# A Winograd up projection whose weight sums are formed by accumulating DMAs instead of VectorE

## The chip, the core and the metric

The kernel runs on one core of a Trainium2 chip. The metric is the device time of one execution in microseconds (us). An execution is profiled on the same core; all times of single instructions below come from that profiled execution and count from the first instruction of its span.

## The reference, cut to what matters

One decoder layer on 512 tokens of width 1024 in float32: two kinds of attention, cross attention to 256 memory tokens, then the MLP, which is all that the change touches:

```
a = square(relu(rms_norm(h, g_mlp) @ w_up))     # w_up:   1024 x 4096
h = h + a @ w_down                              # w_down: 4096 x 1024
return rms_norm(h, g_final)
```

## The kernel before, in words

**Products.** A float32 operand is kept as the sum of two float32r parts, hi and lo, and every matrix product is three matmuls (`mm3`, lines 102 to 104): hi times hi, hi times lo, lo times hi. Weights come in pieces of 128 x 1024 elements (512 KB). A piece is loaded by a DMA of SyncE's queue (`load`, line 122), split by `parts` into hi (a copy on ScalarE, line 109) and lo (a subtraction on VectorE, line 113), and then used by TensorE. The tiles hi and lo have three buffers each, shared by all pieces in the order of their use. So the split of a piece can begin when TensorE has done the piece three places ahead of it, and TensorE has two pieces to work on meanwhile.

**The up projection** is done in eight groups, numbered 0 to 7 here. A group is one 2 x 2 block problem (two blocks of 256 features, two of 512 inputs, two of 256 tokens) done with Winograd's seven products in place of eight. With A11 to A22 the four weight blocks of 512 KB (feature block, input block), the weight operands of the seven products are, in their order

```
p1: A11   p5: S1 = A21 + A22   p2: A12   p6: S2 = S1 - A11   p3: S4 = A12 - S2   p4: A22   p7: S3 = A11 - A21
```

`up_items` (line 967) makes them: each block is loaded once, and the four sums S1, S2, S4 and S3 are `tensor_tensor` instructions of VectorE (lines 983, 991, 995, 1002). S2 takes the place of S1 in the tile `s`. The tiles `blk` and `s` share seven buffers (`BLK`), of which a group takes five. The activation operands (sums of token blocks) are made once, ahead of group 0. `product` (line 1079) is 24 matmuls of 128 x 256; `up_group` adds the products up on VectorE, and `put` squares and splits the result.

**The order.** Groups 0 and 1 run one after the other; groups 2, 4 and 6 are woven with the down projection of an earlier quarter (a product, a piece of `w_down`, a product, and so on; a down piece is 24 matmuls of 128 x 512 in the tiles `mm` and `sc`); groups 3, 5 and 7 stand alone again, each behind a woven one. Products rotate over four PSUM banks named `tr` and `av`. The order on ScalarE, VectorE and GpSimd is set by the framework's scheduler; each engine and each DMA queue then runs its instructions strictly in that order. GpSimd has next to nothing to do in the MLP: the few small instructions of `up_norm` in group 0.

Of the kernel before, what the change touches and what calls it, by code (L numbers as in the profile page):

```python
# [10 lines left out]
F32 = mybir.dt.float32  # L11
# [4 lines left out]
ALU = mybir.AluOpType  # L16
AX = mybir.AxisListType

P = 128
# [4 lines left out]
# pairs of feature tiles of a quarter in the order in which the up projection makes them  # L24
DOWN = (0, 2, 1, 3)
EPS = 1e-6
# PE microseconds of filler work after each half of a step, per unit
# [12 lines left out]
# ROPE_THETA ** (-arange(0, 16, 2) / 16) in float32  # L40
# [5 lines left out]
def two_pi_parts(bits, n):  # L46
    """2 pi as a sum of n floats of the given number of bits each."""
    from decimal import Decimal, getcontext

    getcontext().prec = 60  # L50
    rest = Decimal("6.28318530717958647692528676655900576839433879875021164194988918")
    parts = []
    for _ in range(n):
        e = math.frexp(float(rest))[1]
        unit = Decimal(2) ** (e - bits)
        q = (rest / unit).to_integral_value(rounding="ROUND_DOWN") * unit
        parts.append(float(q))
        rest -= q
    return parts
# [3 lines left out]
def tile_decoder_layer(  # L63
# [24 lines left out]
    nc = tc.nc  # L88
# [10 lines left out]
    # Every matrix product is the sum of three products of parts: a float32 is the  # L99
    # exact sum of two float32r, a = hi + lo, and lo * lo lies below float32's last place.  # L100
# [5 lines left out]
    def split(hi, lo, src, scale=1.0, eng=None):  # L106
        """hi + lo = src * scale; scale is a number or a column of one per partition."""
        if isinstance(scale, float):
            nc.scalar.activation(hi, src, AF.Copy, bias=0.0, scale=scale)  # L109
        else:  # L110
            nc.scalar.activation(hi, src, AF.Identity, bias=0.0, scale=scale)
        if isinstance(scale, float) and scale == 1.0:
            (eng or nc.vector).tensor_tensor(lo, src, hi.bitcast(F32), ALU.subtract)  # L113
        else:
            nc.vector.scalar_tensor_tensor(lo, src, scale, hi.bitcast(F32), ALU.mult, ALU.subtract)

    # Pieces of weights in the order of their use; each is loaded and split some pieces ahead.
# [25 lines left out]
    def proj_n(act, o, n, last=8, ahead=2):  # L143
        """o = (act @ w)^T for the next 128 columns of weights and an activation with features
        first; what the steps cost on TensorE."""
        whi, wlo = take(ahead)
        for c in range(8):
            if c == last:
                yield None
            mm3(o, (whi[:, c, :], wlo[:, c, :]), (act[0][:, c, :n], act[1][:, c, :n]), c == 0, c == 7)  # L150
            yield 1.3e-3 * n
# [5 lines left out]
    def rsqrt(pool, v, n, name, eng=None):  # L157
        """v ** -0.5 for a few columns: a guess from the exponent and three Newton steps."""
        y = pool.tile([P, n], F32, tag=name, name=name)
        t = pool.tile([P, n], F32, tag=name + "_t", name=name + "_t")  # L160
        eng = eng or nc.vector
        eng.tensor_scalar(y.bitcast(I32), v.bitcast(I32), -0.5, float(0x5F3759DF), ALU.mult, ALU.add)
        for _ in range(3):
            eng.tensor_tensor(t, y, y, ALU.mult)
            if eng is nc.vector:
                eng.scalar_tensor_tensor(t, t, -0.5, v, ALU.mult, ALU.mult)
                eng.scalar_tensor_tensor(y, t, 1.5, y, ALU.add, ALU.mult)
            else:
                eng.tensor_tensor(t, t, v, ALU.mult)
                eng.tensor_scalar(t, t, -0.5, 1.5, ALU.mult, ALU.add)  # L170
                eng.tensor_tensor(y, t, y, ALU.mult)
        return y
# [72 lines left out]
    for i in range(2):  # L245
        m = cp.tile([P, P], BF16, name=f"mask{i}")
        nc.gpsimd.memset(m, 0.0)
        # kept where q - k - i >= 0
        nc.gpsimd.affine_select(m, m, pattern=[[-1, P]], compare_op=ALU.is_ge, fill=NEG,
                                base=-i, channel_multiplier=1)  # L250
        masks.append(m)
# [16 lines left out]
    # A query tile holds two heads of 64 features: q[h] has the two parts of head h below each other,  # L268
    # hi in its own rows; k[h] has hi of head h in both halves, k[2] lo of both heads in their rows.
# [72 lines left out]
    # Work that fills TensorE between the steps of the mixers, in its order.  # L342
# [21 lines left out]
    class Mixer:  # L364
        """One step of a mixer: a head of differential attention, or a pair of stick-breaking heads."""
# [5 lines left out]
        def scores(self, i):  # L371
            """Scores of query block i against the keys up to its end, for both halves of the rows."""
# [38 lines left out]
        def transpose(self, i):  # L411
            """Weights of query block i into blocks i, i + 3, ... (one for each key block)."""
# [67 lines left out]
    def by_key(w, j):  # L480
        """Weights of key block j, and the columns of query tokens they go to."""
        b0 = 11 if j == 3 else 4 * j
        n = 2 if j == 3 else 4 - j
        return w[:, b0:b0 + n, :].rearrange("p b q -> p (b q)"), slice(S - n * P, S)
# [60 lines left out]
    # x with features first waits in DRAM for the residual  # L545
# [27 lines left out]
    # TensorE runs at its full clock only after some microseconds of work  # L573
# [43 lines left out]
    # angles, and their remainders by 2 pi in three steps, each exact  # L617
# [17 lines left out]
    # cos(a) = sin(pi / 2 - |a|)  # L635
# [9 lines left out]
    # the queries and keys of the first mixer are an eighth; put_k makes the keys whole again  # L645
# [28 lines left out]
    # lambda  # L674
# [152 lines left out]
    kx = [xp.tile([P, 8, M], F32R, name=f"kx{i}") for i in range(2)]  # L827
    vx = [xp.tile([P, 2, D], F32R, name=f"vx{i}") for i in range(2)]
    for n in range(8):
# [3 lines left out]
        if n == 1:  # L833
            # scale of the queries, folded into the softmax
# [112 lines left out]
    # The up projection is done in 2 x 2 blocks (of features, of inputs, of tokens) with Winograd's seven  # L947
    # products for eight: for W = A11 .. A22 (feature block, input block) and activations B11 .. B22
    # (input block, token block)
    #   S1 = A21 + A22, S2 = S1 - A11, S3 = A11 - A21, S4 = A12 - S2  # L950
    #   T1 = B12 - B11, T2 = B22 - T1, T3 = B22 - B12, T4 = T2 - B21
    #   U2 = A11 B11 + S2 T2, U3 = U2 + S3 T3
    #   C11 = A11 B11 + A12 B21, C12 = U2 + S1 T1 + S4 B22, C21 = U3 - A22 T4, C22 = U3 + S1 T1
# [13 lines left out]
    def up_items(q, g):  # L967
        blk = {}
        c0 = q * 1024 + g * 256

        def block(i, j):
            c = c0 + 512 * i
            return load(w_up[:, 4 * j:4 * j + 4, c:c + 256], ml, "blk", bufs=BLK)

        def p1():
            blk[11] = block(0, 0)
            return parts(blk[11])

        def p5():
            blk[21] = block(1, 0)  # L980
            blk[22] = block(1, 1)
            blk["s"] = ml.tile([P, 4, 256], F32, tag="blk", bufs=BLK, name="s")
            nc.vector.tensor_tensor(blk["s"], blk[21], blk[22], ALU.add)
            return parts(blk["s"])

        def p2():
            blk[12] = block(0, 1)
            return parts(blk[12])

        def p6():  # L990
            nc.vector.tensor_tensor(blk["s"], blk["s"], blk[11], ALU.subtract)
            return parts(blk["s"])

        def p3():
            nc.vector.tensor_tensor(blk[12], blk[12], blk["s"], ALU.subtract)
            return parts(blk[12])

        def p4():
            return parts(blk[22])

        def p7():
            nc.vector.tensor_tensor(blk[11], blk[11], blk[21], ALU.subtract)
            return parts(blk[11])
# [3 lines left out]
    def weave(a, b):  # L1007
        """Steps of two lists in turn."""
        return [x for pair in itertools.zip_longest(a, b) for x in pair if x is not None]

    # the steps of the MLP: products of the up projection beside pieces of the down projection
# [83 lines left out]
    def up_group(u):  # L1095
# [17 lines left out]
        add(u2, product(t2), p1, ALU.add)  # L1113
        add(u4, u2, p5, ALU.add)
        yield
        add(c12, product(b22), u4, ALU.add)
# [4 lines left out]
        add(u2, product(t3), u2, ALU.add)  # L1121
# [32 lines left out]
    def up_norm():  # L1154
# [3 lines left out]
        # relu(r u)^2 = r^2 relu(u)^2 for r > 0: the square of the scale goes onto the down products  # L1158
# [25 lines left out]
    # the sum of squares of a token and acc * g_final over the columns done  # L1184
# [17 lines left out]
    # h = -0.5 (mean + eps), the part of it that is done  # L1202
# [18 lines left out]
    def root(h):  # L1221
        # (-2 h) ** -0.5: a guess from the exponent and three Newton steps
# [9 lines left out]
    def finish(t, cols, r):  # L1232
        """cols: the columns that are still to be multiplied by g_final."""
# [55 lines left out]
```

## Time and profile before

| | |
|---|---|
| three runs | 797.5, 799.82, 801.35 us; median 799.82 us |
| the profiled execution | span 795.6 us from first to last instruction |
| TensorE busy (matmuls) | 769.2 us, 97% of the span |
| VectorE, ScalarE, GpSimd busy | 553.1, 423.9, 104.7 us |
| mean granted TensorE clock | 0.986 of full speed |
| moved by DMAs | 77.98 MB, of it 73.03 MB read from HBM |
| chain that ended last | TensorE 84%, VectorE 9%, ScalarE 3%, DMA 1% |

The profile gives no other time for the profiled execution than its span; the median of the runs is 4.2 us longer, which is taken as what lies around the span. Matmuls overlap in the pipeline, so the duration of a single one (0.28 us for 128 x 256) is longer than the distance to the next (0.12 us): the pace is read from the starts.

### The profile page before, as it was taken

The page shows a single profiled execution, that of the slowest core. Times are in us where ns is not written, and L with a number is a line of the kernel's source. Part 1 is how long each engine was busy: PE and PEld are TensorE (multiplying, and loading weights), DVE is VectorE, ACT ScalarE, POOL GpSimd, SP SyncE. Part 2 cuts the span into 40 slices and gives each one's busy share as a digit, 9 for nine tenths or more (in the row PEclk, how much of TensorE's full clock was granted, in tenths as well). Part 3 has the DMA queues.
Part 4 walks back from the last instruction along what each step waited for, and adds up shares of the span by engine and source line. Part 5 has one row for each costly group of instructions (what it writes and reads, how often), then busy time and mean ns, then how long its engine had stood idle before and what let it go on. Part 6 is the DMA issues. An engine that isn't in the chain of part 4 may idle for free.

```text
span 795.6 us, 11669 instructions
## 1 busy us (share of the span) xinstructions
PE 769.2 (97%) x4552; PEld 668.1 (84%) x4552; DVE 553.1 (70%) x829; ACT 423.9 (53%) x723; POOL 104.7 (13%) x200
## 2 busy tenths in 40 slices
PE   7997999999979999999999999999999999999996
PEld 6886788877867899888888899888988899889885
DVE  3889877689896874445746989556865486647745
ACT  5646655777756554254535788333543454345622
POOL 7166443420050011000000030000000000000000
PEclk9998999999989999999999999999999999999998
DMA  9522111211113446224361044332334233230402
GB/s 267 164 81 79 54 54 54 75 35 56 50 53 118 148 130 188 82 77 133 102 191 53 27 162 131 106 107 79 114 99 127 86 92 121 80 105 1 133 1 106
DMA packets 83977, 77.98 MB, mean 98 GB/s; under 512 B 2545, under 2 KB 70290, under 8 KB 83922
## 3 DMA queue, kind: packets, MB, share of 16 engines
q1 hardware_dynamic: 83120, 76.16, 30.8%
q0 software_dynamic: 160, 0.13, 0.4%
q8 instruction: 36, 0.59, 0.3%
q10 hardware_dynamic: 642, 0.93, 0.3%
q14 instruction: 19, 0.16, 0.1%
HBM read 73.03 MB, written 4.19 MB: 97 GB/s over the span
## 4 chain that ended last, share of the span: by engine, by line
PE 84%; DVE 9%; ACT 3%; DMA 1%; issue 1%; POOL 0%; SPq 0%; DVEq 0%; ACTq 0%
PE mm L102 14%; PE mm L103 13%; PE mm L104 13%; PE av L102 5%; PE av L103 5%; PE av L104 5%; PE sc L102 4%; PE sc L103 4%; PE sc L104 4%; PE tr L102 4%; PE tr L104 4%; PE tr L103 4%; PE tr L422 1%; DMA raw<-in_w_in_dram 1%; PE av L451 1%
## 5 line engine op out<-in xcount | busy, mean ns | idle before, releaser
L109 ACT ACTIVATE hi<-raw 128x1024 fp32r<-128x1024 f32 x92 | 97.3, 1057 | 77.7 <-PE tr L103 15.2
L113 DVE TENSOR_TENSOR lo<-raw,hi 128x1024 fp32r<-128x1024 f32 x80 | 99.6, 1245 | 44.7 <-ACT hi L109 43.4
L109 ACT ACTIVATE hi<-blk 128x1024 fp32r<-128x1024 f32 x40 | 42.4, 1061 | 70.1 <-PE sc L104 48.3
L102 PE MATMUL mm<-a,hi 128*128 128x512 f32 x160 | 66.6, 416 | 0.2
L113 DVE TENSOR_TENSOR lo<-blk,hi 128x1024 fp32r<-128x1024 f32 x40 | 48.7, 1221 | 25.9 <-ACT hi L109 25.9
L103 PE MATMUL mm<-a,hi 128*128 128x512 f32 x160 | 63.3, 395 | 0.0
L104 PE MATMUL mm<-a,lo 128*128 128x512 f32 x160 | 63.2, 395 | 0.0
L102 PE MATMUL mm<-b,hi 128*128 128x512 f32 x128 | 50.2, 393 | 0.0
L104 PE MATMUL mm<-b,lo 128*128 128x512 f32 x128 | 50.0, 390 | 0.0
L103 PE MATMUL mm<-b,hi 128*128 128x512 f32 x128 | 49.8, 389 | 0.0
L102 PE MATMUL av<-a,hi 128*128 128x256 f32 (+1 forms) x144 | 42.7, 296 | 0.0
L103 PE MATMUL av<-a,hi 128*128 128x256 f32 (+1 forms) x144 | 42.7, 296 | 0.0
L104 PE MATMUL av<-a,lo 128*128 128x256 f32 (+1 forms) x144 | 42.6, 296 | 0.0
L102 PEld LDWEIGHTS mm<-a,hi 128*128 128x128 f32 x160 | 30.1, 188 | 8.7 <-issue 1.6
L102 PE MATMUL tr<-a,hi 128*128 128x256 f32 x128 | 36.2, 283 | 0.0
L104 PE MATMUL tr<-a,lo 128*128 128x256 f32 x128 | 36.2, 283 | 0.0
L103 PE MATMUL tr<-a,hi 128*128 128x256 f32 x128 | 36.2, 283 | 0.0
L104 PEld LDWEIGHTS mm<-a,lo 128*128 128x128 f32 x160 | 30.1, 188 | 6.9
L103 PEld LDWEIGHTS mm<-a,hi 128*128 128x128 f32 x160 | 30.2, 189 | 5.9 <-POOL a L726 0.2
L102 PE MATMUL mm<-hi,a 128*128 128x256 f32 x112 | 34.4, 307 | 0.0
L103 PE MATMUL mm<-lo,a 128*128 128x256 f32 x112 | 32.6, 291 | 0.0
L104 PE MATMUL mm<-hi,a 128*128 128x256 f32 x112 | 32.5, 291 | 0.0
(388 smaller groups left out, 2346.5 us busy)
## 6 DMA issues: line engine op xcount, KB each, us to landing
blk<-in_w_up_dram SPq DMA_DIRECT2D x32, 512.0 KB, 3.7
raw<-in_w_down_dram SPq DMA_DIRECT2D x32, 512.0 KB, 3.3
raw<-in_w_in_dram SPq DMA_DIRECT2D x24, 512.0 KB, 3.8
raw<-in_w_xkv_dram SPq DMA_DIRECT2D x16, 512.0 KB, 3.9
raw<-in_w_out_dram SPq DMA_DIRECT2D x8, 512.0 KB, 4.0
raw<-in_w_xq_dram SPq DMA_DIRECT2D x8, 512.0 KB, 4.0
raw<-in_w_xo_dram SPq DMA_DIRECT2D x8, 512.0 KB, 4.1
x<-in_x_dram SPq DMA_DIRECT2D x4, 512.0 KB, 8.4
```

The source lines that it names most:

```text
L102: nc.tensor.matmul(o, l[0], r[0], start=first, stop=False)
L103: nc.tensor.matmul(o, l[0], r[1], start=False, stop=False)
L104: nc.tensor.matmul(o, l[1], r[0], start=False, stop=last)
L109: nc.scalar.activation(hi, src, AF.Copy, bias=0.0, scale=scale)
L113: (eng or nc.vector).tensor_tensor(lo, src, hi.bitcast(F32), ALU.subtract)
L422: nc.tensor.transpose(tr[:, j, :], self.es[i][:, h, j * P:(j + 1) * P], ident)
L451: nc.tensor.matmul(o[:, cols], vj, w, start=(j == 0 and part == 0), stop=(j == 3 and part == 1))
```

## The change

The four sums leave VectorE. A block is loaded into a tile by SyncE's queue as before, and a second DMA, issued on GpSimd's queue with `accum_op=ALU.add`, adds another block from DRAM onto it. Since only additions are used, the signs of the first feature block are turned: S2, S4 and S3 become S1 + A11, A12 + (S1 + A11) and A11 + A21, and three instructions of `up_group` subtract where they added. S1, S2 and S4 now follow each other in one tile, `blk["s"]`; A22 and A11 are loaded a second time. Comments were also removed.

```diff
-        def block(i, j):
+        def at(i, j):
             c = c0 + 512 * i
-            return load(w_up[:, 4 * j:4 * j + 4, c:c + 256], ml, "blk", bufs=BLK)
+            return w_up[:, 4 * j:4 * j + 4, c:c + 256]
+
+        def block(i, j):
+            return load(at(i, j), ml, "blk", bufs=BLK)
+
+        def add(raw, i, j):
+            nc.gpsimd.dma_start(raw, at(i, j), accum_op=ALU.add)
+            return raw

         def p1():
-            blk[11] = block(0, 0)
-            return parts(blk[11])
+            return parts(block(0, 0))

         def p5():
-            blk[21] = block(1, 0)
-            blk[22] = block(1, 1)
-            blk["s"] = ml.tile([P, 4, 256], F32, tag="blk", bufs=BLK, name="s")
-            nc.vector.tensor_tensor(blk["s"], blk[21], blk[22], ALU.add)
+            blk["s"] = add(block(1, 0), 1, 1)
             return parts(blk["s"])

         def p2():
-            blk[12] = block(0, 1)
-            return parts(blk[12])
+            return parts(block(0, 1))

         def p6():
-            nc.vector.tensor_tensor(blk["s"], blk["s"], blk[11], ALU.subtract)
-            return parts(blk["s"])
+            return parts(add(blk["s"], 0, 0))

         def p3():
-            nc.vector.tensor_tensor(blk[12], blk[12], blk["s"], ALU.subtract)
-            return parts(blk[12])
+            return parts(add(blk["s"], 0, 1))

         def p4():
-            return parts(blk[22])
+            return parts(block(1, 1))

         def p7():
-            nc.vector.tensor_tensor(blk[11], blk[11], blk[21], ALU.subtract)
-            return parts(blk[11])
+            return parts(add(block(0, 0), 1, 0))
...
-        add(u2, product(t2), p1, ALU.add)
+        add(u2, product(t2), p1, ALU.subtract)
...
-        add(c12, product(b22), u4, ALU.add)
+        add(c12, product(b22), u4, ALU.subtract)
...
-        add(u2, product(t3), u2, ALU.add)
+        add(u2, u2, product(t3), ALU.subtract)
```

How the instructions stand on VectorE around p6 and p3 of group 1. Before, `s_4678` is the tile of S1 and S2 of this group, `blk_4744` that of A12 and S4, `lo_4777` and `lo_4807` are the lo parts of p6 and p3:

```order
L991 TENSOR_TENSOR s_4678<-s_4678,blk_4644 128x1024
L1121 TENSOR_TENSOR resid_93<-av_4457,resid_93 128x512
L113 TENSOR_TENSOR lo_4747<-blk_4744,hi_4746 128x1024
L1002 TENSOR_TENSOR blk_4644<-blk_4644,blk_4674 128x1024
L1122 TENSOR_TENSOR resid_93<-resid_93,tr_4456 128x512
L1123 TENSOR_TENSOR resid_93<-resid_93 128x512
L995 TENSOR_TENSOR blk_4744<-blk_4744,s_4678 128x1024
L113 TENSOR_TENSOR lo_4777<-s_4678,hi_4776 128x1024
```

and in the changed kernel, where `blk_4675` is the one tile of S1, S2 and S4, and `lo_4775` and `lo_4805` are the lo parts of p6 and p3:

```order
L113 TENSOR_TENSOR lo_4745<-blk_4742,hi_4744 128x1024
L1123 TENSOR_TENSOR resid_93<-resid_93,tr_4453 128x512
L1124 TENSOR_TENSOR resid_93<-resid_93 128x512
L113 TENSOR_TENSOR lo_4775<-blk_4675,hi_4774 128x1024
L113 TENSOR_TENSOR b1_2770<-resid_93,b0_2769 128x2x256 x2
L1111 TENSOR_TENSOR resid_93<-tr_4453,resid_93 128x512
L1114 TENSOR_TENSOR resid_93<-av_4454,resid_93 128x512
L1115 TENSOR_TENSOR resid_93<-resid_93 128x512
L113 TENSOR_TENSOR lo_4805<-blk_4675,hi_4804 128x1024
L113 TENSOR_TENSOR lo_4840<-blk_4837,hi_4839 128x1024
```

The sums are gone, and p6 and p3 are split from the same tile, so that the DMA that makes S4 must wait until `lo_4775` has read S2.

GpSimd's queue in the MLP held only `up_norm` before (from line 1159 on; the two rows ahead belong to the cross attention):

```order
L841 TENSOR_SCALAR rx_2771<-rsh_3168 128x4
L842 TENSOR_SCALAR nrx_2772<-rsh_3168 128x4
L1159 TENSOR_SCALAR ssh_4096<-ssh_4096 128x4
L162 TENSOR_SCALAR rsm2_4728<-ssh_4096 128x4
L164 TENSOR_TENSOR rsm2_t_4729<-rsm2_4728 128x4
```

and now, from the end of `up_norm` on, holds the additions. `blk_4675` is the sum tile of group 1, `blk_4976` of group 2, `blk_5431` of group 3, `blk_5700` of group 4; `blk_5299` and `blk_5593` are S3 of groups 2 and 3:

```order
L1162 TENSOR_TENSOR r2_4095<-rsm2_4726 128x4
L981 DMA blk_4675<-in_w_up_dram 128x4x256
L981 DMA blk_4976<-in_w_up_dram 128x4x256
L981 DMA blk_4675<-in_w_up_dram 128x4x256
L981 DMA blk_5299<-in_w_up_dram 128x4x256
L981 DMA blk_5431<-in_w_up_dram 128x4x256
L981 DMA blk_4976<-in_w_up_dram 128x4x256 x2
L981 DMA blk_5593<-in_w_up_dram 128x4x256
L981 DMA blk_5700<-in_w_up_dram 128x4x256
L981 DMA blk_5431<-in_w_up_dram 128x4x256 x2
```

The first sum of the next group (S1 of group 2, of group 4) now stands directly ahead of S4 of group 1 and of S2 of group 3 in the same queue.

## Rows read from the trace of the kernel before

**Rows 1.** The page: its span, and busy time, share and instructions by engine.

```profile
span 795.6 us, 11669 instructions
...
PE 769.2 (97%) x4552; PEld 668.1 (84%) x4552; DVE 553.1 (70%) x829; ACT 423.9 (53%) x723; POOL 104.7 (13%) x200
```

**Rows 2.** Table by stage: stretch, length, busy per engine (count), clock, DMA share, GB/s.

```profile
500.00:520.00 20.00, 20.00 (x123) 17.96 (x122) 10.27 (x11) 8.06 (x10) 0.00 (x0) 1.00 0.28 93
...
640.00:660.00 20.00, 20.00 (x170) 20.00 (x170) 16.46 (x19) 11.91 (x16) 0.00 (x0) 1.00 0.37 106
```

**Rows 3.** TensorE's waits over the span: us in total, times, longest.

```profile
PE av L451 <- DVE wt L113: 5.2, 1, 5.2
PE sc L378 <- DVE rt L296: 4.5, 1, 4.5
```

**Rows 4.** Groups by line, VectorE: busy and mean; idle before, by releaser.

```profile
L983 DVE TENSOR_TENSOR s<-blk 128x1024 f32<-128x1024 f32 x8 | 9.8, 1224 | 4.6 <-DMA blk<-in_w_up_dram 3.9 <-DVE lo L113 0.4
```

**Rows 5.** VectorE in order of time: start, us, instruction [idle before].

```profile
444.86 1.23 DVE L113 TENSOR_TENSOR lo<-s,hi 128x1024 fp32r<-128x1024 f32 x1 [0.17 <-ACT hi L109]
...
470.15 1.23 DVE L113 TENSOR_TENSOR lo<-s,hi 128x1024 fp32r<-128x1024 f32 x1 [0.24 <-ACT hi L109]
...
551.28 1.22 DVE L113 TENSOR_TENSOR lo<-s,hi 128x1024 fp32r<-128x1024 f32 x1 [1.00 <-ACT hi L109]
...
562.41 1.22 DVE L113 TENSOR_TENSOR lo<-blk,hi 128x1024 fp32r<-128x1024 f32 x1 [0.20 <-ACT hi L109]
...
593.52 1.23 DVE L113 TENSOR_TENSOR lo<-s,hi 128x1024 fp32r<-128x1024 f32 x1 [4.47 <-ACT hi L109]
```

**Rows 6.** ScalarE in order of time, at the same places.

```profile
453.08 1.06 ACT L109 ACTIVATE hi<-s 128x1024 fp32r<-128x1024 f32 x1 [0.27 <-PE tr L103]
...
474.74 1.06 ACT L109 ACTIVATE hi<-s 128x1024 fp32r<-128x1024 f32 x1 [1.78 <-PE av L103]
...
558.38 1.06 ACT L109 ACTIVATE hi<-s 128x1024 fp32r<-128x1024 f32 x1 [1.69 <-PE tr L103]
...
561.31 1.06 ACT L109 ACTIVATE hi<-blk 128x1024 fp32r<-128x1024 f32 x1 [1.39 <-PE av L103]
...
600.72 1.06 ACT L109 ACTIVATE hi<-blk 128x1024 fp32r<-128x1024 f32 x1 [2.13 <-PE sc L104]
```

**Rows 7.** TensorE: the first matmul of p3 in groups 0, 1 and 3.

```profile
463.31 0.28 PE L102 MATMUL tr<-a,hi 128*128 128x256 f32 x1
...
483.17 0.28 PE L102 MATMUL av<-a,hi 128*128 128x256 f32 x1
...
566.89 0.28 PE L102 MATMUL tr<-a,hi 128*128 128x256 f32 x1
```

**Rows 8.** The page: DMA queues (packets, MB, share); issues (KB, us to landing).

```profile
q1 hardware_dynamic: 83120, 76.16, 30.8%
q0 software_dynamic: 160, 0.13, 0.4%
...
blk<-in_w_up_dram SPq DMA_DIRECT2D x32, 512.0 KB, 3.7
...
lv<-in_lambda_q_dram POOLq DMA_DIRECT2D x2, 32.0 KB, 7.5
```

**Rows 9.** GpSimd in order of time, near the start.

```profile
2.14 0.99 POOL L526 DMA_DIRECT2D pos_i<-in_positions_dram  x1
```

**Rows 10.** Table by stage, behind TensorE's two long waits.

```profile
63.80:68.90 5.10, 5.09 (x23) 4.57 (x24) 4.86 (x7) 3.52 (x8) 3.97 (x3) 0.50 0.00 0
68.90:72.00 3.10, 3.10 (x22) 2.84 (x21) 2.99 (x6) 2.21 (x7) 2.70 (x3) 0.76 0.02 5
...
232.70:236.20 3.50, 3.41 (x11) 3.12 (x12) 3.50 (x7) 0.58 (x1) 0.41 (x2) 0.50 0.00 0
236.20:239.00 2.80, 2.80 (x20) 2.61 (x18) 1.61 (x4) 1.45 (x3) 0.41 (x2) 0.74 0.00 0
```

More of the change, by code (lines that the diff above doesn't have):

```diff
@@ L969, in up_items @@
         c0 = q * 1024 + g * 256
+        def at(i, j):
+            c = c0 + 512 * i
+            return w_up[:, 4 * j:4 * j + 4, c:c + 256]
         def block(i, j):
-            c = c0 + 512 * i
-            return load(w_up[:, 4 * j:4 * j + 4, c:c + 256], ml, "blk", bufs=BLK)
+            return load(at(i, j), ml, "blk", bufs=BLK)
+        def add(raw, i, j):
+            nc.gpsimd.dma_start(raw, at(i, j), accum_op=ALU.add)
+            return raw
         def p1():
-            blk[11] = block(0, 0)
-            return parts(blk[11])
+            return parts(block(0, 0))
         def p5():
-            blk[21] = block(1, 0)
-            blk[22] = block(1, 1)
-            blk["s"] = ml.tile([P, 4, 256], F32, tag="blk", bufs=BLK, name="s")
-            nc.vector.tensor_tensor(blk["s"], blk[21], blk[22], ALU.add)
+            blk["s"] = add(block(1, 0), 1, 1)
             return parts(blk["s"])
         def p2():
-            blk[12] = block(0, 1)
-            return parts(blk[12])
+            return parts(block(0, 1))
         def p6():
-            nc.vector.tensor_tensor(blk["s"], blk["s"], blk[11], ALU.subtract)
-            return parts(blk["s"])
+            return parts(add(blk["s"], 0, 0))
         def p3():
-            nc.vector.tensor_tensor(blk[12], blk[12], blk["s"], ALU.subtract)
-            return parts(blk[12])
+            return parts(add(blk["s"], 0, 1))
         def p4():
-            return parts(blk[22])
+            return parts(block(1, 1))
         def p7():
-            nc.vector.tensor_tensor(blk[11], blk[11], blk[21], ALU.subtract)
-            return parts(blk[11])
+            return parts(add(block(0, 0), 1, 0))
         return [p1, p5, p2, p6, p3, p4, p7]
```

## The prediction, made before the changed kernel ran

> **What bounds the kernel now.** I read the page first: TensorE is busy for 769.2 of 795.6 us, VectorE for 553.1, GpSimd for 104.7 [rows 1]. A share over the whole span says little about one stage, so the table by stage is next: in the MLP TensorE is busy without a break, 20.00 us in each stretch of 20, in a woven one (500 to 520) as in one with a group that stands alone (640 to 660); VectorE is at 10.3 and 16.5 there [rows 2]. The list of TensorE's waits agrees: its two long ones, 5.2 and 4.5 us, lie in the mixers, and none names an instruction of the MLP [rows 3]. So here TensorE is the bound, and work taken from VectorE shortens nothing unless TensorE was waiting for it.
>
> **What is removed.** Four sums in each of eight groups. The row of S1 stands for all four lines: 8 instructions, 1.224 us each [rows 4]. 32 x 1.224 = 39 us of VectorE, worth 0 on the path, since TensorE waited for none of them. The turned signs cost nothing: the same instructions with another operation.
>
> **What is added, and where it could be felt.** 72 transfers of 512 KB in place of 32, of which 32 are additions on GpSimd's queue. What matters is the time L from the moment an addition may start to the moment its sum is there. S1 and S3 are made early, from loads that nothing holds up. But S2 is added onto S1 in its own tile, so its addition waits until p5's lo part is made; S4 is added onto S2 and waits for p6's lo part. That is a chain of two additions and two splits, which in a group that stands alone runs against TensorE's pace, with nothing but products in between. A split takes 2.32 us: hi starts at 561.31 [rows 6], lo ends at 562.41 + 1.22 = 563.63 [rows 5]. The moments that frame the chain, from the trace:
>
> - group 1: p5's lo ends at 470.15 + 1.23 = 471.38 [rows 5]; TensorE frees the buffers of p6 at 474.74 [rows 6]; p3's product starts at 483.17 [rows 7].
> - group 3: 552.50, 558.38 and 566.89 [rows 5 to 7]. Groups 5 and 7, also behind a woven group, are taken to be the same.
> - group 0: 446.09, 453.08, 463.31 [rows 5 to 7]; its earlier pieces are the long ones of the output projection, which gives more time.
> - woven groups: in group 4 p6's lo runs from 593.52 to 594.75 [rows 5], its hi some 1.06 us before it, and p3's hi comes two pieces of work later at 600.72 [rows 6]; so two pieces take 8.3 us, and p3's product, again two later, starts near 609.0. With 594.75 + L + 2.32 that leaves room for an L of 11.9 us.
>
> p6's split starts at the later of its free buffers and (p5's lo + L); S4's addition starts 2.32 later; p3 is ready after a further L + 2.32. What exceeds the start of p3's product is a gap on TensorE.
>
> **How long is L?** The trace of before has no accumulating DMA. The lower end is a plain load of the same block, 3.7 us from issue to landing [rows 8]. The upper end is the pace of the only transfers that GpSimd's queue issued: 0.13 MB in 0.4% of the time of 16 engines [rows 8], that is 3.2 us of all of them or 41 GB/s, by which 0.524 MB take 12.8 us; these were small pieces in the crowded start, where 32 KB took 7.5 us to land [rows 8]. I go up from the lower end, since the size is the same: 3.7, and 1.0 for the issue on GpSimd, as long as the one DMA there with 512 pieces took [rows 9], and once more the 1.7 us that the 16 engines need for 0.524 MB (30.8% of 795.6 us for 76.16 MB [rows 8]), because the destination must be read too. That is 6.4; with S1 of the next group directly ahead in the queue of S4 of group 1 and of S2 of group 3, I take **L = 7 us**.
>
> With that, group 1: 471.38 + 7 = 478.38; + 2.32 + 7 + 2.32 = 490.02, against 483.17: a gap of 6.85 us. Group 3: 552.50 + 7 = 559.50; + 11.64 = 571.14, against 566.89: 4.25 us, three times 12.75. Group 0: 453.09 + 11.64 = 464.73, against 463.31: 1.42. Sum **21.0 us**. While p3's split waits at the head of ScalarE's and VectorE's queues, the activations of earlier products wait behind it, but TensorE stands as well, and p4 and p7 need only a split each afterwards, so I add nothing for them.
>
> To this comes the clock. After each of the two long waits of before, the granted clock fell to 0.50, 1.2 GHz, and TensorE worked at that level for 5.1 + 1.5 = 6.6 us and for 3.4 + 1.5 = 4.9 us (the 1.5 each from the stretch with a mean of 0.76 and 0.74) [rows 10]. Half of it is lost: 3.3 and 2.4, on average 2.9 us. The gap in group 1 is longer than both waits and gets 2.9. The gaps of 4.25 are a little shorter than any that the trace shows with this effect, so they get half, 1.45 each. Together 7.3 us.
>
> Sum: 21.0 + 7.3 = 28.3 us more. On the profiled execution that is 795.6 + 28.3 = 823.9 of span; the median of the runs is 799.82, 4.2 above that span, so **828 us**.
>
> The ends: at L = 3.7, group 1 has 471.38 + 3.7 = 475.08, + 8.34 = 483.42, a gap of 0.25, and the others none: 0.3 us in all. At L = 12.8, 18.5 + 3 x 15.9 + 13.0 = 79 us, and five drops of the clock, 14.5: some 894 us. An effect of 0.5%, 4 us, is about what a measurement of this kernel can tell from none; it is reached at L = 4.6, where group 1 loses 2.1 and the three others 0.7 each.
>
> **Rivals.**
>
> *A, the additions fit into the slack: not slower.* Decides below L = 4.6. For it speaks the plain load with its 3.7 us, and that the DMA engines are idle for most of the MLP (shares of 0.28 and 0.37 [rows 2]). Against it: the second read of 512 KB, and the software queue, whose 32 KB landed after 7.5 us [rows 8]. Time: 800 to 804. The Trainium skill ("DMA: Bandwidth & Descriptors", section "Anatomy of one DMA — SWDGE (gpsimd) path") gives GpSimd's DMAs about 2.0 us plus bytes by 436 GB/s, 3.2 us for this size as an estimate; with an issue of 1.0 us the sum would be some 2 us, no change. The trace agrees with that figure for plain loads of SyncE (3.7) and shows it for no addition.
>
> *B, the DMA engines become the bound: much slower.* In the 20 us of a group that stands alone there now fall five loads and four additions. At 1.7 us a load and, read twice, 3.4 us an addition, that is 22 us of all 16 engines, where a share of 0.37, 7.4 us, stood before [rows 2]. Then transfers queue, L rises to 9 and beyond, and gaps of 8 to 16 us stand in groups 3, 5 and 7: 855 to 894. Against it: loads may run ahead into the seven buffers during the woven groups, which have three times as long. The same page ("Issuing engines are not separate DMA queues") says that all queues run on the same 16 engines; by that rule the 32 additions take from the loads whatever queue they are on.
>
> *C, VectorE was closer to the bound than it looks: faster.* Without the sums p6 of group 1 is split earlier, and ScalarE and VectorE have room. But a gain needs a wait on TensorE, and there is none [rows 2, 3]. To count as faster it would have to give back 4 of the 39 us: 790 to 796.
>
> **Chances.** The forecast (L from 4.6 to 9) 0.55, B 0.20, A 0.22, C 0.03. Slower by over 0.5%: 0.75. Within 0.5%: 0.22. Faster: 0.03. The range leaves out the lower part of A and the upper part of B: from 803 (L = 4.4, 3.2 us) to 871 (L = 10.6: 8.6 + 14.1 + 3 x 11.5 = 57, and 14.5 for the clock). The forecast's own range is 804 to 855 (L = 9: 5.4 + 10.9 + 3 x 8.3 = 41, and 14.5).
>
> **What would show it.** In the profile after: 32 issues of `blk` on GpSimd's queue with a median landing time near 7 us; no rows of the four sums on VectorE; among TensorE's waits p3's products (in banks `tr` and `av`) waiting for `lo`, five of them, about 21 us in total, the longest in group 1; a granted clock of 0.5 behind it; no waits in woven groups; some 21 MB more moved. Landing times near 4 us and no such waits would prove A; waits in woven groups too, and a DMA share near 1 in the others, B. The prediction is wrong at its root if TensorE's gaps lie elsewhere than at p6 and p3 of groups that stand alone.

## The result, and the profile after

The changed kernel takes **827.06 us** (median of four runs, 825.7 to 828.19), the kernel before 798.66 (four runs, 795.47 to 801.35): a ratio of 1.036, 95% interval 1.033 to 1.039. The profiled execution after took 826.97 us with a span of 825.1; the one before has a span of 795.6. In every execution on record with both figures the time is 1.7 to 1.9 us longer than the span. So the 4.2 us that stood ahead of the prediction as what lies around the span are too much by 2.3: the profiled execution was a shorter one than the median.

The page after answers to [rows 1] and [rows 8]:

```profile
span 825.1 us, 11767 instructions
...
PE 782.4 (95%) x4552; PEld 678.4 (82%) x4552; DVE 520.2 (63%) x797; ACT 423.2 (51%) x723; POOL 146.3 (18%) x232
...
q1 hardware_dynamic: 87344, 80.36, 30.8%
q0 software_dynamic: 17056, 16.91, 14.0%
...
L981 POOL DMA_DIRECT2D blk<-in_w_up_dram x32 | 41.3, 1306 | 394.3 <-DVE lo L113 172.0
...
blk<-in_w_up_dram SPq DMA_DIRECT2D x40, 512.0 KB, 4.9
blk<-in_w_up_dram POOLq DMA_DIRECT2D x32, 512.0 KB, 6.1
```

VectorE gave up 32 instructions and 32.9 us (553.1 to 520.2) and GpSimd took on 41.6; TensorE is busy 13.2 us longer with the same 4552 matmuls, most of it the lower clock (a mean of 0.973 against 0.986). The 32 additions landed 6.1 us after their issue (median), and the plain loads 4.9 instead of 3.7.

TensorE's waits over the span answer to [rows 3]: the two long ones of the mixers are still there (not shown), and these are new or longer (us in total, times, longest):

```profile
PE av L102 <- ACT hi L109: 6.8, 3, 2.8
...
PE tr L422 <- DVE e L399: 5.2, 2, 4.1
...
PE tr L102 <- ACT hi L109: 3.3, 2, 1.7
PE av L104 <- DVE lo L113: 2.0, 3, 0.8
PE tr L104 <- DVE lo L113: 1.9, 3, 0.8
```

The four rows of `hi` and `lo` lie in the MLP: 14.0 us in all, where before there was nothing. (L422 is in a mixer; more on it at the end of the section on why the prediction was right.) TensorE in order of time shows where they stand; here p6 and p3 of group 1, and p3 of group 3:

```profile
487.56 0.58 PE L102 MATMUL av<-t,hi 128*128 128x256 f32 x1 [2.80 <-ACT hi L109]
...
488.82 0.58 PE L104 MATMUL av<-t,lo 128*128 128x256 f32 x1 [0.46 <-DVE lo L113]
...
496.25 0.39 PE L102 MATMUL av<-a,hi 128*128 128x256 f32 x1 [2.36 <-ACT hi L109]
...
497.51 0.49 PE L104 MATMUL av<-a,lo 128*128 128x256 f32 x1 [0.76 <-DVE lo L113]
...
584.45 0.39 PE L102 MATMUL tr<-a,hi 128*128 128x256 f32 x1 [1.68 <-ACT hi L109]
...
585.71 0.39 PE L104 MATMUL tr<-a,lo 128*128 128x256 f32 x1 [0.76 <-DVE lo L113]
```

Each product waits twice: first for the hi part, then, after 0.5 to 0.8 us of work, for the lo part. Groups 5 and 7 repeat group 3 (idle for 2.41 and 2.39 us in place of 2.44), and group 0 has one gap of 0.41. Before, no product of the MLP waited. The profile counts a gap from the end of the last matmul, but a next one would have started ahead of that end (matmuls of 0.28 us start 0.12 apart), so a gap delays TensorE by more than its idle time; the delays below are read from the starts.

The table by stage answers to [rows 2] and [rows 10]: group 1, a woven group, group 3, and then two stretches right behind the gaps.

```profile
480.00:500.00 20.00, 13.62 (x79) 12.62 (x78) 8.28 (x10) 9.09 (x14) 1.49 (x2) 0.77 0.71 128
500.00:520.00 20.00, 20.00 (x139) 18.77 (x139) 11.27 (x14) 12.04 (x17) 3.83 (x3) 0.97 0.97 225
580.00:600.00 20.00, 17.56 (x127) 16.90 (x126) 12.90 (x16) 12.24 (x17) 3.33 (x3) 0.91 0.82 181
...
487.40:490.80 3.40, 2.77 (x11) 2.48 (x12) 2.44 (x4) 2.67 (x6) 1.28 (x1) 0.50 0.23 36
...
586.40:589.80 3.40, 3.40 (x18) 3.40 (x17) 3.32 (x5) 1.56 (x3) 0.00 (x0) 0.50 0.83 257
```

TensorE's 20.00 became 13.62 and 17.56 in the groups that stand alone, and stayed 20.00 in the woven one, although the DMA share there went to 0.97. Behind the gaps of groups 3, 5 and 7 stand 3.4 us at a granted clock of 0.50 each; in group 1 it is 6.8 us from 487.4 and 3.4 from 497.6.

**The delay by group.** Take the start of the same product in both traces, counted from the first product of the MLP (450.07 us before, 453.46 after); what it is later after the change is the delay so far. Its steps are, in us:

| kernel | group 0 | 1 | 3 | 5 | 7 | woven 2, 4, 6 | sum |
|---|---|---|---|---|---|---|---|
| the change | 0.86 | 11.46 | 4.49 | 4.45 | 4.43 | 0 | 25.7 |
| alone_only | 1.02 | 9.9 | 5.0 | 4.75 | 4.4 | 0 | 25.1 |
| s4_only | 3.58 | 6.1 | 6.15 | 6.7 | 2.5 | 0 | 25.0 |
| s2_only | 0 | 1.75 | 0 | 0 | 0 | 0 | 1.75 |
| s1_s3_only, woven_only, signs_only | 0 | 0 | 0 | 0 | 0 | 0 | 0 |
| p3_last | 0 | 4.06 | 0 | 0 | 0 | 0 | 4.1 |
| s4_from_s2 | 0 | 5.44 | 0 | 0 | 0 | 0 | 5.4 |
| plain_gpsimd | 0 | 5.53 | 0.68 | 0.62 | 0.57 | 0 | 7.4 |

The rows below the first belong to the experiments.

### The profile page after: what moved, and what is told of

Its sections match the earlier page's. It is cut to its first block, busy times and chain, and to the rows that moved or that the text cites. A ratio compares the mean times of both kernels' runs of the same rounds, so it can differ in the third digit from the quotient of the medians.

```text
span 825.1 us, 11767 instructions
## 1 busy us (share of the span) xinstructions
PE 782.4 (95%) x4552; PEld 678.4 (82%) x4552; DVE 520.2 (63%) x797; ACT 423.2 (51%) x723; POOL 146.3 (18%) x232
## 3 DMA queue, kind: packets, MB, share of 16 engines
q0 software_dynamic: 17056, 16.91, 14.0%
## 4 chain that ended last, share of the span: by engine, by line
PE 74%; DVE 10%; DMA 8%; ACT 5%; issue 2%; POOL 1%; SPq 0%; DVEq 0%; ACTq 0%; POOLq 0%
PE mm L102 13%; PE mm L103 13%; PE mm L104 13%; DMA blk<-in_w_up_dram 7%; PE sc L104 4%; PE sc L102 4%; PE sc L103 4%; PE av L104 3%; PE av L102 3%; PE av L103 3%; DVE lo L113 3%; PE tr L104 3%; PE tr L102 3%; PE tr L103 2%; ACT hi L109 2%
## 5 line engine op out<-in xcount | busy, mean ns | idle before, releaser
L109 ACT ACTIVATE hi<-blk 128x1024 fp32r<-128x1024 f32 x56 | 58.7, 1056 | 118.6 <-PE sc L104 56.2
L113 DVE TENSOR_TENSOR lo<-blk,hi 128x1024 fp32r<-128x1024 f32 x56 | 68.0, 1223 | 73.4 <-ACT hi L109 73.4
L981 POOL DMA_DIRECT2D blk<-in_w_up_dram x32 | 41.3, 1306 | 394.3 <-DVE lo L113 172.0
L102 PE MATMUL av<-a,hi 128*128 128x256 f32 (+1 forms) x144 | 44.5, 309 | 4.0 <-ACT hi L109 4.0
L104 PE MATMUL av<-a,lo 128*128 128x256 f32 (+1 forms) x144 | 44.5, 309 | 1.5 <-DVE lo L113 1.5
L103 PE MATMUL av<-a,hi 128*128 128x256 f32 (+1 forms) x144 | 44.0, 306 | 0.0
L102 PE MATMUL tr<-a,hi 128*128 128x256 f32 x128 | 37.7, 295 | 3.3 <-ACT hi L109 3.3
L104 PE MATMUL tr<-a,lo 128*128 128x256 f32 x128 | 37.9, 296 | 1.9 <-DVE lo L113 1.9
L103 PE MATMUL tr<-a,hi 128*128 128x256 f32 x128 | 37.6, 294 | 0.0
L102 PE MATMUL mm<-hi,a 128*128 128x256 f32 x112 | 34.1, 304 | 0.0
L102 PEld LDWEIGHTS av<-a,hi 128*128 128x128 f32 x144 | 28.9, 201 | 5.6 <-ACT hi L109 4.5
```

What stands on the lines that cost most here:

```text
L102: nc.tensor.matmul(o, l[0], r[0], start=first, stop=False)
L103: nc.tensor.matmul(o, l[0], r[1], start=False, stop=False)
L104: nc.tensor.matmul(o, l[1], r[0], start=False, stop=last)
L981: nc.gpsimd.dma_start(raw, at(i, j), accum_op=ALU.add)
```

## The experiments

Theory: time is lost only through the chain of two additions and two splits in groups that stand alone, where p3's product comes before S4 is split. Rivals: every addition costs something wherever it stands (25.7 / 32 = 0.8 us each), or the turned signs and the other loads cost it. Each of the nine kernels was measured beside the kernel before on the same chip; there were three chips, on which the median of the kernel before was 796.36 to 797.84 us.

The experiments decide per group (`u`) and sum whether a DMA or VectorE forms it; the sums on VectorE use the turned signs too (`add2` is VectorE's `tensor_tensor`):

```diff
         def p6():
-            return parts(add(blk["s"], 0, 0))
+            if "S2" in how:
+                add(blk["s"], 0, 0)
+            else:
+                add2(blk["s"], blk["s"], blk[11], ALU.add)
+            return parts(blk["s"])
```

S1, S4 and S3 are switched in the same way; `how` is `HOW(u)`, and each experiment gives its set.

**signs_only: the signs turned, no addition by DMA.**

```diff
+    HOW = lambda u: set()
```

> All four sums on VectorE again, but with the turned signs (pure additions). Chain theory (the added time is the chain from S1 to S2 to S4 in the groups that stand alone): nothing is left of it, 797 to 802 us, as before. Rival, the DMAs as such (32 additions and 21 MB more cost 28 us in all, about 0.9 us for each addition, wherever it stands): the same, 797 to 802, since no addition is left. If the turned signs or the order that the scheduler makes of them cost something, it shows here alone.

Measured: 795.78 us against 797.55, ratio 0.999 (0.997 to 1.002); no delay in any group. That is 1.2 us below the expected range, but the same as before. The signs are free, as costed.

**woven_only and alone_only: the 12 additions of groups 2, 4 and 6, and the 20 of the others.**

```diff
+    HOW = lambda u: {"S1", "S2", "S4", "S3"} if u in (2, 4, 6) else set()
```

```diff
+    HOW = lambda u: set() if u in (2, 4, 6) else {"S1", "S2", "S4", "S3"}
```

> All four sums by accumulating DMAs in the woven groups 2, 4 and 6 only; on VectorE in the groups that stand alone. Chain theory: between p6's split and p3's product of a woven group lie more than 12 us, enough for a landing time of 6.1 us: 797 to 803 us, with 12 additions. Rival, a cost of each addition wherever it stands (28 us for 32): 809.

> All four sums by accumulating DMAs in the groups that stand alone (0, 1, 3, 5, 7) only; on VectorE in the woven ones. Chain theory: nearly the whole cost, 820 to 829 us, with 20 additions; a little less than with all if group 1 suffers from the first additions of group 2, which now are missing. Rival (0.9 us for each of 20): 816.

Measured: woven_only 795.49 us (below the range, which counted from 797) against 796.36, ratio 0.9995 (0.997 to 1.002); alone_only 821.22, ratio 1.032 (1.028 to 1.036). In woven_only TensorE has no row of waits for `hi` or `lo`, and in its table by stage TensorE fills a stretch of 20 us in which two additions are issued:

```profile
480.00:500.00 20.00, 20.00 (x149) 19.03 (x148) 15.63 (x20) 13.31 (x19) 2.58 (x2) 1.00 0.86 216
```

A price per addition would have made woven_only 9.6 us slower (12 x 0.8), and is out. The whole delay comes from the groups that stand alone: 25.1 of 25.7 us.

**s1_s3_only, s2_only, s4_only: which link of the chain.**

```diff
+    HOW = lambda u: {"S1", "S3"}
```

```diff
+    HOW = lambda u: {"S2"}
```

```diff
+    HOW = lambda u: {"S4"}
```

> Only S1 and S3 are made by accumulating DMAs; S2 and S4 on VectorE. Chain theory: neither waits for a split, both are made well ahead: 797 to 802 us, with 16 additions. Rival (0.9 us for each of 16): 813.

> Only S2 is made by an accumulating DMA; S1, S4 and S3 on VectorE. Chain theory: in group 3 the addition may start at 552.5 and lands at 558.6, when p6's buffers come free at 558.4, so no gap; in group 1 471.4 + 6.1 = 477.5, + 2.32 = 479.8 against p6's product at 480.35, just in time: 797 to 803 us. Rival (0.9 us for each of 8 additions): 806, the same as with S4 alone.

> Only S4 is made by an accumulating DMA, onto the tile of S2; S1, S2 and S3 on VectorE. Chain theory with a landing time of 6.1 us, as the profile after shows: the addition starts behind p6's lo, in group 3 at 560.95, so p3 is ready at 560.95 + 6.1 + 2.32 = 569.4 against 566.89, a gap of 2.5 us and some 2 us for the clock, three times; group 1 some 3.5 + 2.9, group 0 1.4: about 21 us, 816 to 824 us, most of the whole. Rival (0.9 us for each of 8 additions): 806.

Measured: s1_s3_only 797.52 us, ratio 1.000 (0.998 to 1.003); s2_only 799.16, ratio 1.001 (0.9985 to 1.004); s4_only 821.93, ratio 1.030 (1.024 to 1.036); all against 797.55. Sixteen additions made ahead of their use cost nothing. The eight S4 alone cost 25.0 us, as much as all 32, although here only one addition stands in the chain. TensorE's waits in s4_only:

```profile
PE tr L102 <- ACT hi L109: 6.8, 3, 3.3
PE av L102 <- ACT hi L109: 5.2, 2, 2.8
```

That one addition costs as much as two has a cause that we had not foreseen. By our own sum one addition in group 3 gives 558.38 + 2.32 + 6.4 + 2.32 = 569.42 against 566.89, a gap of 2.5 us, and not 4. VectorE in order of time, p6 of group 3 in s4_only (its hi part was ready at 568.46):

```profile
569.31 1.23 DVE L998 TENSOR_TENSOR s<-blk 128x1024 f32<-128x1024 f32 x1 [1.74 <-issue]
570.45 1.22 DVE L113 TENSOR_TENSOR lo<-s,hi 128x1024 fp32r<-128x1024 f32 x1
```

S1 of the next group, in this kernel a sum on VectorE, stands ahead of p6's lo part and makes it 2 us late (570.45 in place of 568.46), and the DMA of S4 waits for that lo part. Group 7, which no group follows, has no such S1 and loses 2.5 us, as the sum says, where groups 3 and 5 lose over 6; that bears the cause out. So S4 alone is enough to break the pace, but s4_only overstates its share of the change, and its median inside the expected range owes something to luck.

Group 0 of s4_only shows another thing. TensorE stood idle there for 2.29 + 0.76 = 3.05 us ahead of 466.35, longer than in group 3 of the changed kernel, and the granted clock stayed at 1.00 behind it:

```profile
466.50:480.00 13.50, 13.50 (x115) 13.50 (x116) 11.92 (x14) 9.06 (x13) 0.45 (x1) 1.00 0.45 134
```

So a gap of this length does not always bring the clock down; what else decides was not tried.

**p3_last: all 32 additions, p3's product moved behind p4 and p7.**

```diff
-        return [p1, p5, p2, p6, p3, p4, p7]
+        return [p1, p5, p2, p6, p4, p7, p3]
```

with the lines that use the products in `up` moved in the same way.

> All 32 additions as in the changed kernel, but the product p3 and its piece come last in each group, behind p4 and p7: two products more, 5.7 us, for S4 to be made. Chain theory: group 3's p3 is ready near 569.3 and due at 572.6, so the gaps of groups 0, 3, 5 and 7 vanish; in group 1 the late S2 (8.8 us to land beside the S1 of group 2) stays, 3.3 us and its clock: 799 to 807 us. Rival, DMA traffic or additions as such: 820 and more, since they are all still there.

Measured: 802.65 us against 796.36, ratio 1.007 (1.004 to 1.010). Groups 0, 3, 5 and 7 lose nothing any more, with the same 32 additions landing in 6.4 us. The MLP's only waits that are left are these, both at p6 of group 1, ahead of the moved product:

```profile
PE av L102 <- ACT hi L109: 1.4, 1, 1.4
...
PE av L104 <- DVE lo L113: 0.8, 1, 0.8
```

**s4_from_s2: S4 made by adding S2's tile, by DMA, onto the tile of A12.** The addition no longer overwrites S2, so it does not wait for p6's lo part: it may go while p6 is split. The edit in short (`blk[12]` is the tile of A12, which `p2` keeps):

```diff
-            return parts(add(blk["s"], 0, 1))
+            nc.gpsimd.dma_start(blk[12], blk["s"], accum_op=ALU.add)
+            return parts(blk[12])
```

> S4 is formed by adding the tile of S2 from SBUF onto the tile of A12, so its DMA waits for S2's landing and not for p6's split; the other sums as in the changed kernel. Chain theory: the 2.3 us of a split go out of the chain: group 3's p3 is ready at 558.6 + 6.1 + 2.3 = 567.0 against 566.9, so the gaps of groups 3, 5 and 7 shrink from 2.4 to 0 to 0.5 us; group 1 keeps its late S2 and loses 5 to 9 us: 802 to 811. Rival, additions as such: 825 or more.

Measured: 803.86 us against 796.36, ratio 1.008 (1.005 to 1.010). Again groups 0, 3, 5 and 7 lose nothing; p6 of group 1, and p3 by a little, are left. The page's issues:

```profile
blk<-in_w_up_dram POOLq DMA_DIRECT2D x24, 512.0 KB, 7.7
...
blk<-blk POOLq DMA_DIRECT2D x8, 512.0 KB, 4.6
```

With one split less in the chain, and an addition from SBUF of 4.6 us, the chain fits; which of the two did more was not tried apart. Two edits that share nothing but the chain each take away some 20 us: that the chain is the cause is shown.

**plain_gpsimd: the same 32 transfers as plain copies.** The additions are left out, so the sums are not formed; the rest stands.

```diff
-            nc.gpsimd.dma_start(raw, at(i, j), accum_op=ALU.add)
+            nc.gpsimd.dma_start(raw, at(i, j))
```

> The changed kernel with its 32 transfers on GpSimd's queue as plain copies: the addition itself is left out, so that the sums are not formed; queue, issue, sizes, order and waits are the same. Of the 6.1 us that an addition took, 1.3 are GpSimd's issue, and a plain load on SyncE's queue took 3.7. If the rest is the addition's (a read of the destination in front of each write), the copies land in 4 to 5 us, the chain is 2 to 4 us shorter, group 3, 5 and 7 stand without gaps, group 1 keeps at most a small one: 797 to 803 us. If it is the queue's (what GpSimd must do for 512 pieces, and how the engines take them), the copies land in 5.7 to 6.2 us, and groups 3, 5 and 7 keep gaps of 1.6 to 2.5 us: 815 to 825 us.

Measured: 805.54 us against 797.84, ratio 1.009 (1.006 to 1.012), a little above the range of the first case and far below the second. The page:

```profile
q0 software_dynamic: 4768, 16.91, 7.1%
...
L981 POOL DMA_DIRECT2D blk<-in_w_up_dram x32 | 24.1, 755 | 396.3 <-DVE lo L113 176.8
...
blk<-in_w_up_dram POOLq DMA_DIRECT2D x32, 512.0 KB, 4.4
```

A copy lands in 4.4 us, an addition in 6.1. GpSimd's issue is 0.54 us longer for the addition (1.29 against 0.75). The queue's time on the engines halves: 7.1% of 808.0 less the 3.2 us of before is 54 us, 1.7 per copy; 14.0% of 825.1 less 3.2 is 112 us, 3.5 per addition. So it is the addition and not GpSimd's queue that makes the chain too long: without it groups 3, 5 and 7 lose 0.6 us each in place of 4.5. Group 1 keeps 5.5, for a reason of its own (below).

No version that ran beats the kernel before. The best, woven_only and signs_only, equal it, since TensorE is without a wait in the MLP there.

## Why the prediction was right

**The direction and the place** were right. TensorE was the bound, so VectorE's relief was worth nothing (signs_only and woven_only: no change), and the loss stands at p3 of the groups that stand alone. The signs of being right came, two of them in another form: TensorE's waits name first `hi` and then `lo`, and the additions' median landing is 6.1 us and not near 7. What the reading of [rows 5 to 7] missed is that in group 1 p6 waits too: by its own sum p6's lo part is there at 478.38 + 2.32 = 480.70, and p6's product started at 480.35.

**L, taken as 7 us, was 6.4.** Group 3 after the change, link by link: VectorE, GpSimd and ScalarE in order of time (one fence each).

```profile
567.00 1.23 DVE L113 TENSOR_TENSOR lo<-blk,hi 128x1024 fp32r<-128x1024 f32 x1 [1.00 <-ACT hi L109]
...
575.70 1.23 DVE L113 TENSOR_TENSOR lo<-blk,hi 128x1024 fp32r<-128x1024 f32 x1 [1.81 <-ACT hi L109]
```

```profile
568.52 1.29 POOL L981 DMA_DIRECT2D blk<-in_w_up_dram  x1 [11.19 <-DVE lo L113]
577.22 1.29 POOL L981 DMA_DIRECT2D blk<-in_w_up_dram  x1 [7.41 <-DVE lo L113]
```

```profile
574.61 1.06 ACT L109 ACTIVATE hi<-blk 128x1024 fp32r<-128x1024 f32 x1 [2.20 <-DMA blk<-in_w_up_dram]
...
583.34 2.00 ACT L109 ACTIVATE hi<-blk 128x1024 fp32r<-128x1024 f32 x2 [5.65 <-DMA blk<-in_w_up_dram]
```

p5's lo ends at 568.23, the addition is issued at 568.52, p6's split starts at 574.61: 6.38 us. p6's lo ends at 576.93, the issue follows at 577.22, p3's split starts at 583.34: 6.41. That is the 6.4 that the parts had given (a plain load, the issue, the second read). The runs bear out the sum and not each part: the issue took 1.29 us and not 1.0, and an addition 1.7 us more than a copy. The 6.4 was rounded up to 7 for the next group's S1 ahead in the queue. In group 3 nothing stood ahead: that S1 was issued at 556.03, long before.

**The gap in groups 3, 5 and 7** was forecast as 4.25 us. Read from the starts of TensorE's matmuls, in the changed kernel and then before, it is 2.97 in group 3:

```profile
585.93 0.28 PE L102 MATMUL tr<-a,hi 128*128 128x256 f32 x1
...
589.94 0.28 PE L102 MATMUL av<-t,hi 128*128 128x256 f32 x1
```

```profile
567.25 0.28 PE L102 MATMUL tr<-a,hi 128*128 128x256 f32 x1
...
569.74 0.28 PE L102 MATMUL av<-t,hi 128*128 128x256 f32 x1
```

The first row of each is p3's fourth matmul, right behind both waits, the second p4's first. Group 3 began 15.71 us later than before (3.38 ahead of the MLP, 12.33 in groups 0 and 1); p3's fourth matmul is 18.68 later, so the two waits cost 2.97; p4 is 20.20 later, so 1.52 more went in the slow stretch. Groups 5 and 7 give 2.94 and 2.92 for the waits. With L = 6.4 the sum of the prediction gives 552.50 + 2 x (6.4 + 2.32) = 569.94 against 566.89, 3.05: so the term that was sized wrong here is L, and the rest of the chain was right.

**The clock** was put at 1.45 us each and took 1.52: 3.4 us at a granted clock of 0.50, in which a matmul followed the last after 0.21 us in place of 0.12. That it fits is luck: 1.45 was half of the cost seen behind the long waits, taken because 4.25 us was shorter than any wait of before, and the gap was shorter still. In group 0 of s4_only 3.05 us of idle time cost nothing of this kind.

**Group 1** was forecast as 6.85 + 2.9 = 9.75 us and took 11.46. Its chain took 3.2 us more than forecast, 10.0: so much later does TensorE get p3's lo part. With the measured L (10.4 and 6.4, below) the prediction's sum gives 471.38 + 10.4 + 2.32 + 6.4 + 2.32 = 492.82 against 483.17, 9.65, most of the 10.0. The 3.4 us at 0.50 behind p3 took the other 1.5, in place of 2.9. The 6.8 us at 0.50 behind p6's gap add nothing to that, since TensorE then waits for S4 anyway. Its S2 is the late one. GpSimd, then ScalarE, in order of time:

```profile
477.11 0.20 POOL L1162 TENSOR_TENSOR r<-rsm 128x4 f32<-128x4 f32 x1
477.59 2.62 POOL L981 DMA_DIRECT2D blk<-in_w_up_dram  x2 [0.28 <-DVE resid L1122]
489.07 1.28 POOL L981 DMA_DIRECT2D blk<-in_w_up_dram  x1 [8.86 <-DVE lo L113]
```

```profile
486.46 1.06 ACT L109 ACTIVATE hi<-blk 128x1024 fp32r<-128x1024 f32 x1 [5.72 <-DMA blk<-in_w_up_dram]
...
495.14 2.95 ACT L109 ACTIVATE hi<-blk 128x1024 fp32r<-128x1024 f32 x3 [2.34 <-DMA blk<-in_w_up_dram]
```

p5's lo part ended at 476.08, but S2 stands behind the last step of `up_norm` in GpSimd's queue and went only at 477.59, 1.5 us later, with S1 of group 2 right behind it, and took 8.8 us to land. The prediction had put the place behind `up_norm` at nothing. And in that stretch the DMA engines are full (shares of 1.05 and 1.15), as the table by stage shows.

```profile
470.00:478.00 8.00, 8.00 (x69) 7.87 (x68) 7.18 (x9) 6.38 (x9) 6.60 (x14) 1.00 1.05 338
478.00:484.80 6.80, 6.76 (x58) 6.56 (x56) 1.66 (x3) 1.64 (x3) 2.21 (x2) 1.00 1.15 214
```

So here L was 10.4 for S2 and 6.4 for S4 (489.07 to 495.14, and 0.3 ahead of it). This is what is left in p3_last, s4_from_s2 and plain_gpsimd, where the same S2 is late. What the neighbour in the queue is worth shows in alone_only, where S1 of group 2 is a sum on VectorE. GpSimd, then ScalarE, at S2 of group 1:

```profile
472.14 1.30 POOL L982 DMA_DIRECT2D blk<-in_w_up_dram  x1 [0.28 <-DVE resid L1148]
```

```profile
479.52 1.06 ACT L109 ACTIVATE hi<-blk 128x1024 fp32r<-128x1024 f32 x1 [4.24 <-DMA blk<-in_w_up_dram]
```

From the issue to the split it is 7.4 us there, 8.9 in the changed kernel and 6.8 in s2_only. So the neighbour, in the queue and on the DMA engines, is worth some 1.5 us, about the difference of group 1 in the table (11.46 against 9.9). In group 3 an addition landed in 6.0 us; what is left above that is put down to the other additions and loads, which was not tried apart.

**Group 0** was forecast as 1.42 us and took 0.86. **The woven groups** took none, as forecast: their room went up to an L of 11.9.

**The sum** in the MLP is 25.7 us where 28.3 were forecast, and the time, 827.06 against 828, agrees better than its parts do. The waits came to 19.7 us in place of 21.0 (10.0 in group 1, 8.83 in groups 3, 5 and 7 together, 0.86 in group 0), the clock to 6.0 in place of 7.3; in the waits 3.2 too few for group 1 stand against 3.9 too many for groups 3, 5 and 7. And the 2.3 us too many around the span stand against 3.4 us of the profiled difference that lie ahead of the MLP (453.46 - 450.07), in code that did not change. That all this comes to 1 us is luck. The 3.4 us hang on the row of L422 above (4.1 in place of 1.1 us), and this on one instruction. VectorE and GpSimd in the trace of before:

```profile
70.50 0.35 DVE L398 TENSOR_SCALAR e<-e,es 128x256 f32<-128x256 f32 x1
```

```profile
70.77 4.90 POOL L113 TENSOR_TENSOR lo<-raw,hi 128x1024 fp32r<-128x1024 f32 x2 [0.32 <-POOL q L113]
```

and after:

```profile
69.64 2.55 DVE L398 TENSOR_SCALAR e<-e,es 128x256 f32<-128x256 f32 x1
```

```profile
69.69 4.70 POOL L113 TENSOR_TENSOR lo<-raw,hi 128x1024 fp32r<-128x1024 f32 x2
```

The same instruction takes 0.35 us when it starts 0.27 us ahead of GpSimd's, and 2.55 when it starts 0.05 ahead. The long form stands in 3 of the 11 profiles of this study (the change, s4_from_s2, plain_gpsimd), and a lead of 0.05 us is found with the long form and (in alone_only) with the short one, so what decides is not shown. This fits chance, but all three have 32 transfers on GpSimd's queue, as one of the other eight has, so that a link to the change is not excluded.

**Rival A** (the additions fit) failed on L. The Trainium skill ("DMA: Bandwidth & Descriptors", section "Anatomy of one DMA — SWDGE (gpsimd) path") gave an estimate of 3.2 us for the size; here a copy took 4.4 and an addition 6.1, and the measurement decides. The prediction called SyncE's plain loads, 3.7 us, an agreement with that figure; they lay 0.5 above it, on another queue.

**Rival B** (the DMA engines become the bound) expected the engines to be full in the groups that stand alone. The share was 0.97 in a woven group and up to 1.15 in group 1, and in the 20 us around the end of group 3 it was 0.82; outside group 1 the additions of the chain kept their pace (both of group 3 landed in 6.0 us). **Rival C** found no wait to remove.

## What to carry to other kernels

Moving work from an engine to a DMA saves nothing where nobody waited for that engine; what counts is the latency that the DMA puts into a chain. An addition in place makes its tile a serial resource: write, read by the splits, write again; before doing it, lay the chain against the pace of the bound engine, and either put the last consumer later (p3_last) or add into another tile (s4_from_s2). Where the additions have room (woven_only), they are free, and also worth nothing here.

## What the runs showed of the hardware that was not expected

- In groups 3, 5 and 7 of the changed kernel TensorE was idle for 2.4 us (in two pieces of 1.7 and 0.8) and then had 3.4 us at a granted clock of 0.50: 2.9 to 3.0 us for the waits and 1.5 for the clock. The length of the gap does not settle it: 2.2 us in p3_last were followed by such a stretch, 3.05 us in group 0 of s4_only were not.
- An accumulating DMA of 512 KB took 3.5 us of all 16 engines against 1.7 for a copy, 1.29 us of issue against 0.75, and 384 more packets each ((17056 - 4768) / 32). It landed in 6.1 us (median), 8.8 beside many loads, and in 4.6 when its source was in SBUF.
- One VectorE instruction of unchanged code took 0.35 us in eight profiles and 2.55 in three, each time with a GpSimd instruction starting 0.04 to 0.27 us behind it; what decides between the two is open.
